# A token-mixing trunk on one core: ScalarE empties the banks of r, k, v and of the convolution's input, the scan's output moves into another tile, modulation steps are split, and the steps stand in a new order

## The chip, the cores and the metric

The kernel runs on one core of a Trainium2 chip. The metric is device microseconds of one execution, the median of three runs. TensorE (PE in the profile) multiplies matrices and writes PSUM, VectorE (DVE) and ScalarE (ACT) do elementwise work and read PSUM, GpSimd (POOL) does elementwise work in SBUF, and SyncE (SP) issues most DMAs.

## The reference, cut to what matters

One layer on 512 tokens of width 1024, in fp32. The hidden state `h` is projected by one wide matrix to the inputs of three branches; then the gated result goes through `w_out`, and a squared-ReLU MLP of width 4096 follows.

```python
h = _rms_norm(x, norm_mix_gain[l]) * (1.0 + sc_m) + sh_m
proj = h @ w_comb                                   # 1024 -> 7424 columns
rwkv_in = _token_shift(proj[..., :N_SHIFT], mu_shift[l])   # p + (p_prev - p) * mu
conv_in = proj[..., N_SHIFT:N_SHIFT + 2 * D_CONV]
gates = jax.nn.sigmoid(proj[..., N_SHIFT + 2 * D_CONV:N_COLS])
y_a, v_first = _rwkv7_time_mix(rwkv_in, ...)        # r, k, v, decay, a, g; a state per head, step by step
y_b = _conformer_conv(conv_in, ...)                 # u1 * sigmoid(u2), 31 taps per channel, layer norm, silu
merged = jnp.concatenate([y_a, y_b], axis=-1) * gates
x = x + gt_m * (merged @ w_out[l])
h = _rms_norm(x, norm_ffn_gain[l]) * (1.0 + sc_f) + sh_f
x = x + gt_f * (jnp.square(jax.nn.relu(h @ w_ff_in[l])) @ w_ff_out[l])
return _rms_norm(x, final_gain)
```

## The kernel before, in words

**Projections.** Channels lie on the 128 partitions and the 512 tokens along the free axis. Each projection of 128 columns (`proj`) loads its weights, splits them into a high and a low half (`hi` cast on ScalarE, L151; `lo` subtracted on GpSimd or, where the step carries a "v", on VectorE, L152), and runs 24 matmuls of 128x512 into one PSUM bank: for each of 8 blocks of the inner dimension high times high (L175), high times the low half of h (L176) and low times high (L177). The pool of banks for projections has two (tag `pp`), so a third projection starts only when the first one's bank has been read by all that read it.

**Who empties a bank.** For r, k and v, `shift` reads the bank twice: ScalarE writes `(1-mu)*p` to SBUF (L469), then VectorE adds `mu*p` of the token before, read from the bank (L470). In `conv_tile`, ScalarE takes tanh of `ps_u2` (L779), and VectorE multiplies by `ps_u1`, read from its bank (L781). So VectorE's turn decides when these banks come free.

**The scan.** The 16 heads form 8 pairs and 4 quarters of two pairs. `rkv_pair` and `prep_pair` make a pair's operands, among them `tr` (L543), the sum over a head's channels `pb` (a matmul, L545) and its product with v, `bo` (L547). `products`, `solve` (rank-one steps on VectorE, L602 into `tmp`, L604 from `X`), `merge_inverses` (into a tile `RT` whose corner GpSimd clears, L636) and `scan` follow for each quarter; the scan's output `yq` is normalized in `group_norm` and goes to DRAM. The convolution's 30 taps (`conv_taps`, L788) are VectorE instructions of 128x512, started by ScalarE's `cz` (L786); four transposes (`pz`, L793) and `bn_stats` follow.

**The tail of this part.** `gate_a` multiplies the scan's output with its gate (gate tanh L819, a small matmul `pg` L821 with weights `wg`), `gate_b` does so for the convolution (`z`, with a Silu on ScalarE), results are reloaded, and `wo_step` runs one sixteenth of `w_out`. A modulation half (`mod_half`, then four small matmuls in `mod_cols`) sums eight rows of the conditioning matrix on VectorE. The MLP behind it is not touched.

**What sets the order.** The string `ORDER` lists the steps: U a convolution projection pair, R a pair's r, k, v, I products, V solve, O scan operands, M merge, S scan, Y group norm, T taps, N the convolution's norm, G and B the gates, L a reload, W a step of `w_out`, A a modulation half, Q the gate's spread. The number behind a colon moves a step's instructions ahead in the priorities of the framework's list scheduler, which then fixes the instruction order of every engine when the kernel is built; "v" puts the step's `lo` on VectorE.

Of the kernel before, what the change touches and what calls it, by code (L numbers as in the profile page):

```python
# [8 lines left out]
F32 = mybir.dt.float32  # L9
# [9 lines left out]
P = 128  # L19
T = 512  # L20
# [43 lines left out]
def tile_rwkv7_conformer(  # L64
# [143 lines left out]
    def mod_half(dst, seg, h, eng):  # L208

        n, tag = (3, "aacc") if x1 else (1, "w1")  # L210
        acc = tpool[0].tile([P, 512], F32, tag=tag, name=f"aacc{seg}{h}", bufs=1)
        for k in range(KT):
            mod_part(acc, seg, h, k, eng, n)
        return acc
# [32 lines left out]
    pq = cq.enter_context(tc.tile_pool(name="pq", bufs=1, space=PSUM, reuse_waits="tile"))  # L247
    early = {}
    lo_eng = [G]

    with tc.tile_pool(name="e1", bufs=1) as e1, tc.tile_pool(name="e2", bufs=2) as e2:
        xt = e1.tile([P, NT, D], F32, name="xt")
# [32 lines left out]
        ss = e1.tile([P, NT], F32, name="ss")  # L285
        rs = e1.tile([P, NT], F32, name="rs")
        sst = e1.tile([P, NT], F32, name="sst")
        sq = e1.tile([P, D], F32, name="sq")
        for tt in range(NT):
            S.activation(sq, xt[:, tt, :], AF.Square, accum_out=ss[:, tt:tt + 1])  # L290
        rstd_rows(rs, ss, 1.0 / D, 1e-6, sst)
# [165 lines left out]
    with ExitStack() as c1:  # L457
# [50 lines left out]
        def prep_pair(j, rt, kt, vv, sg, WA):  # L508
# [33 lines left out]
            V.tensor_tensor(AR[:, :, C:P], chunks(rt), Pt[:, :, 1:65], op=ALU.mult)  # L542
            V.scalar_tensor_tensor(rt, rt, VEC["r_k"][:, jc], kt, op0=ALU.mult, op1=ALU.mult)  # L543
            pb = pq.tile([P, T], F32, tag="m", name=f"pb{j}", bufs=2)
            PE.matmul(pb, blk1, rt, start=True, stop=True)  # L545
            bo = tp.tile([P, T], F32, tag="w1", name=f"bo{j}")
            V.tensor_tensor(bo, pb, vv, op=ALU.mult)  # L547
# [83 lines left out]
        def merge_inverses(q, d1, d2):  # L631


            RT = xq.tile([P, 16, C], F32, tag="RT", name=f"RT{q}", bufs=2)
            for pr in range(2):
                G.memset(RT[64 * pr + 32:64 * pr + 64, :, 0:32], 0.0)  # L636
            W = xq.tile([P, 7, 8, 32], F32, tag="U", name=f"W{q}")
# [42 lines left out]

        def scan(q, prs, RVs, RT):

            yq = qp.tile([P, NCHK, 2, C], F32, tag="yq", name=f"yq{q}")
            st = qp.tile([P, NCHK, 2, 6], F32, tag="st", name=f"st{q}")
            HP = [slice(0, 64), slice(64, 128)]
            HEADS = [(p, e) for e in range(2) for p in range(2)]
# [87 lines left out]
        def conv_tile(j):  # L774
            ps2 = proj(U2 + j * P, f"u2_{j}")
            tp = tpool[0]
            gl = tp.tile([P, CW - 1 + T], F32, tag="gl", name=f"gl{j}", bufs=2)
            G.memset(gl[:, 0:CW - 1], 0.0)
            S.activation(gl[:, CW - 1:], ps2, AF.Tanh, scale=0.5)  # L779
            ps1 = proj(U1 + j * P, f"u1_{j}")  # L780
            V.scalar_tensor_tensor(gl[:, CW - 1:], gl[:, CW - 1:], 1.0, ps1, op0=ALU.add, op1=ALU.mult)  # L781
            return gl

        def conv_taps(j, gl):
            cz = tpool[0].tile([P, T], F32, tag="cz", name=f"cz{j}")
# [27 lines left out]
        def gate_a(j):  # L813
            tp = tpool[0]
            wg = tp.tile([P, P], F32, tag="wg", name=f"wg{j}")
            nc.sync.dma_start(out=wg, in_=w_gate_up[0][:, j * P:(j + 1) * P])
            ps = proj(GA + j * P, f"ga{j}")
            ga = tp.tile([P, T], F32, tag="ga", name=f"gat{j}")
            S.activation(ga, ps, AF.Tanh, scale=0.5)  # L819
            pg = pp.tile([P, T], F32, tag="o", name=f"pg{j}")  # L820
            PE.matmul(pg, wg, sgl, start=True, stop=True)  # L821
            V.scalar_tensor_tensor(ga, ga, 1.0, pg, op0=ALU.add, op1=ALU.mult)
            gy = tp.tile([P, T], F32, tag="gy", name=f"gy{j}")
            nc.sync.dma_start(out=gy, in_=yad[j])
            V.scalar_tensor_tensor(ga, gy, VEC["gn_bias"][:, j:j + 1], ga, op0=ALU.add, op1=ALU.mult)
            merged(j, ga, 1.0)
# [165 lines left out]
        def step(op):  # L992
# [14 lines left out]
            elif k == "Y":  # L1007
                group_norm(i, quarters[i], *scans[i])
                if i == 3:
                    enter_tail()  # L1010
            elif k == "U":
                scans["gl", i] = conv_tile(i)
            elif k == "T":
                conv_taps(i, scans.pop(("gl", i)))
            elif k == "G":
                gate_a(i)
            elif k == "N":
                scans["cn"] = conv_norm()
            elif k == "B":
                gate_b(i, *scans["cn"])  # L1020
            elif k == "L":
                reload()
            elif k == "A":
                seg, h = 2 + i // 2, i % 2
                acc = mod_half(modt[seg - 2], seg, h, V)
                mod_cols(pp, "o", modt[seg - 2], acc, seg, h)
            elif k == "Q":
                spread(tail["m2"], tail["p2"], "m", gate[0], modt[0], "gm")
            elif k == "W":
                wo_step(int(wn[0] == 16))  # L1030
# [142 lines left out]
```

## Time and profile before

| | |
|---|---|
| median of 3 runs | 1107.88 us (1107.52, 1107.88, 1110.65) |
| profiled execution, its own time | 1106.56 us |
| its span | 1104.8 us |
| mean granted TensorE clock | 0.971 of full speed |
| TensorE busy | 1011.8 us (92% of the span) |
| VectorE busy | 772.9 us (70%) |
| ScalarE busy | 496.3 us (45%) |
| GpSimd busy | 181.2 us (16%) |

The span runs from the first to the last instruction in the profile; the execution's own time is 1.8 us more. A busy share is a mean over the whole span; the projections and the scan lie in the first half of it, and the MLP, which fills TensorE without a gap, in the second.

### The profile page before, as it was taken

To read this page: it belongs to the slowest core of one execution; us is meant where nothing else is said; L and a number is where in the kernel's file an instruction comes from. 1 tells how busy PE (TensorE), PEld (TensorE's weight loads), DVE (VectorE), ACT (ScalarE), POOL (GpSimd) and SP (SyncE) were. 2 spreads that over 40 slices of the span, in tenths; PEclk is the share of its full clock that TensorE was granted. 3 is DMA by queue.
4 is the path that set the end of the run, shared out by engine and by line. 5 is a ranking of instruction groups with operands and counts; after the bars stand their busy time and mean duration, and the time that the engine had idled before them with its cause. 6 is when DMAs were issued, how large, how long until landed. Compare 5 with 4: busy or idle time off the path is not lost.

```text
span 1104.8 us, 18962 instructions
## 1 busy us (share of the span) xinstructions
PE 1011.8 (92%) x7061; PEld 777.7 (70%) x7061; DVE 772.9 (70%) x1525; ACT 496.3 (45%) x980; POOL 181.2 (16%) x188
## 2 busy tenths in 40 slices
PE   3999889998999799996996998999999999999995
PEld 1877666666667576664664776788788888888884
DVE  4869996899569897898665776776555445445557
ACT  5546455745765367344352343363224323423432
POOL 2113044233314441301012022100000000000012
PEclk9999999999999899997898999999999999999998
DMA  9522333222214322323257785623523333323331
GB/s 333 177 72 85 94 86 98 57 60 58 90 37 134 100 60 83 88 75 118 82 180 232 227 264 162 192 84 111 156 87 96 94 92 100 96 94 98 96 105 76
DMA packets 178215, 127.82 MB, mean 116 GB/s; under 512 B 43033, under 2 KB 146891, under 8 KB 178123
## 3 DMA queue, kind: packets, MB, share of 16 engines
q1 hardware_dynamic: 178123, 126.62, 38.1%
q8 instruction: 55, 0.90, 0.3%
q14 instruction: 37, 0.30, 0.1%
HBM read 113.73 MB, written 12.85 MB: 115 GB/s over the span
## 4 chain that ended last, share of the span: by engine, by line
PE 49%; DVE 28%; DMA 10%; ACT 6%; issue 5%; SPq 1%; POOL 1%; DVEq 0%; ACTq 0%; POOLq 0%
DVE cz L788 9%; PE ps_fi L177 5%; PE ps_fi L176 5%; PE ps_fi L175 5%; PE acc_fo L1048 4%; PE acc_fo L1047 4%; PE acc_fo L1046 4%; DMA ar<-in_ada_w_dram 3%; DVE aacc L222 2%; DVE X L604 2%; PE pA L185 2%; DVE tmp L602 2%; DMA mr<-mgd 2%; PE ps_u L177 1%; PE ps_u L176 1%
## 5 line engine op out<-in xcount | busy, mean ns | idle before, releaser
L788 DVE SCALAR_TENSOR_TENSOR cz<-gl,cw,cz 128x512 f32<-128x512 f32 x240 | 199.0, 829 | 3.4 <-ACT cz L786 0.3
L175 PE MATMUL ps_fi<-hh,hi_fi 128*128 128x512 f32 (+1 forms) x288 | 105.7, 367 | 0.0
L176 PE MATMUL ps_fi<-hl,hi_fi 128*128 128x512 f32 (+1 forms) x288 | 105.6, 367 | 0.0
L177 PE MATMUL ps_fi<-hh,lo_fi 128*128 128x512 f32 (+1 forms) x288 | 105.4, 366 | 0.0
L1046 PE MATMUL acc_fo<-hi_fo,fh 128*128 128x512 f32 x256 | 101.2, 395 | 0.0
L1047 PE MATMUL acc_fo<-lo_fo,fh 128*128 128x512 f32 x256 | 101.0, 395 | 0.0
L1048 PE MATMUL acc_fo<-hi_fo,fl 128*128 128x512 f32 x256 | 100.9, 394 | 0.0
L152 DVE TENSOR_TENSOR lo_fo<-raw_fo,hi_fo 128x512 fp32r<-128x512 f32 x64 | 44.2, 691 | 77.0 <-ACT hi_fo L151 76.9
L151 ACT CAST hi_fo<-raw_fo 128x512 fp32r<-128x512 f32 x64 | 39.7, 621 | 108.4 <-PE acc_fo L1048 86.9
L152 DVE TENSOR_TENSOR lo_fi<-raw_fi,hi_fi 128x512 fp32r<-128x512 f32 x64 | 43.9, 690 | 48.1 <-ACT hi_fi L151 47.1
L151 ACT CAST hi_fi<-raw_fi 128x512 fp32r<-128x512 f32 x64 | 39.8, 622 | 76.9 <-PE ps_fi L176 48.8
L1064 POOL TENSOR_TENSOR x<-x,fgain 128x512 f32<-128x512 f32 x4 | 5.5, 1393 | 375.9 <-ACT sq L1058 375.9
L222 DVE SCALAR_TENSOR_TENSOR aacc<-ar,cact,aacc 128x512 f32<-128x512 f32 x56 | 51.6, 922 | 13.8 <-DMA ar<-in_ada_w_dram 13.4
L177 PEld LDWEIGHTS ps_fi<-hh,lo_fi 128*128 128x128 f32 x288 | 54.3, 189 | 8.7
L176 PEld LDWEIGHTS ps_fi<-hl,hi_fi 128*128 128x128 f32 x288 | 54.3, 189 | 8.6
L175 PEld LDWEIGHTS ps_fi<-hh,hi_fi 128*128 128x128 f32 x288 | 54.3, 189 | 8.6
L152 POOL TENSOR_TENSOR lo_u<-raw_u,hi_u 128x512 fp32r<-128x512 f32 x28 | 40.6, 1458 | 94.6 <-ACT hi_u L151 40.7
L1048 PEld LDWEIGHTS acc_fo<-hi_fo,fl 128*128 128x128 f32 x256 | 48.2, 188 | 11.1
L1047 PEld LDWEIGHTS acc_fo<-lo_fo,fh 128*128 128x128 f32 x256 | 48.2, 188 | 10.9
L1046 PEld LDWEIGHTS acc_fo<-hi_fo,fh 128*128 128x128 f32 x256 | 48.2, 188 | 10.9
L175 PE MATMUL ps_u<-hh,hi_u 128*128 128x512 f32 x128 | 53.3, 416 | 2.3 <-DVE lo L470 2.3
L177 PE MATMUL ps_u<-hh,lo_u 128*128 128x512 f32 x128 | 54.6, 427 | 0.3 <-POOL lo_u L152 0.3
(386 smaller groups left out, 2495.4 us busy)
## 6 DMA issues: line engine op xcount, KB each, us to landing
ar<-in_ada_w_dram SPq DMA_DIRECT2D x64, 256.0 KB
raw_fi<-in_w_ff_in_dram SPq DMA_DIRECT2D x64, 256.0 KB
raw_fo<-in_w_ff_out_dram SPq DMA_DIRECT2D x64, 256.0 KB
araw<-in_ada_w_dram SPq DMA_DIRECT2D x8, 1024.0 KB
raw_u<-in_w_in_dram SPq DMA_DIRECT2D x32, 256.0 KB
raw_wo<-in_w_out_dram SPq DMA_DIRECT2D x32, 256.0 KB
raw_k<-in_w_in_dram SPq DMA_DIRECT2D x16, 256.0 KB
raw_v<-in_w_in_dram SPq DMA_DIRECT2D x16, 256.0 KB
```

The lines of the kernel that those rows point to most:

```text
L151: S.copy(hi, raw)
L152: (eng or V).tensor_tensor(lo, raw, hi.bitcast(F32), op=ALU.subtract)
L175: PE.matmul(ps[:, ts_], wh[:, i, :], mh[:, k, ts_], start=first, stop=False, skip_group_check=True)
L176: PE.matmul(ps[:, ts_], wh[:, i, :], ml[:, k, ts_], start=False, stop=False, skip_group_check=True)
L177: return PE.matmul(ps[:, ts_], wl[:, i, :], mh[:, k, ts_], start=False, stop=(k == KT - 1), skip_group_check=True)
L185: last_mm[0] = PE.matmul(*a, **kw).ins
L222: eng.scalar_tensor_tensor(acc, a, cact[:, k:k + 1], acc, op0=ALU.mult, op1=ALU.add)
L602: V.tensor_tensor(tv, X[:, 0:n, s:s + 1].to_broadcast([P, n, m]), U[:, s:s + 1, s + 1:16].to_broadcast([P, n, m]), op=ALU.mult)
L788: V.scalar_tensor_tensor(cz, gl[:, w:w + T], cw[:, w * KT + j:w * KT + j + 1], cz, op0=ALU.mult, op1=ALU.add)
L1046: PE.matmul(acc[tt], fh[:, k, ts_], wh, start=(n == 0), stop=False)
L1047: PE.matmul(acc[tt], fh[:, k, ts_], wl, start=False, stop=False)
L1048: return PE.matmul(acc[tt], fl[:, k, ts_], wh, start=False, stop=(n == KT - 1))
```

## The change

ScalarE copies the bank of each r, k and v projection into a new tile `ev` (two buffers), and VectorE reads `ev` in its place; the same for `ps_u1` with `evu`. That is 24 + 8 ScalarE copies of 128x512 more, and 32 VectorE instructions that read two SBUF tiles in place of a bank and a tile. The scan's output becomes the second half of the inverses' tile RT, which is twice as wide, so that the eight memsets on GpSimd clear twice the columns. `x1`, which shares RT's two buffers, is loaded when these are free. Step A is split into A (the sum on VectorE, with two buffers in the tail) and C (the four matmuls). `fill` can put spare matmuls (high times high, 128x512, the result is never read) ahead of a step; the new order asks for 8 and 6 of them, at two W steps. Some steps of `ORDER` change place and many their number or their "v": on balance one `lo` instruction fewer falls to VectorE, while R1's six go to GpSimd early on and four of U6's come to VectorE later.

```diff
-    "U1:0v R0:0v R1:0v I0 U4 R2:0v R3 V0 I1:200 U3:50 T1:500 M0 O0 T4 S0:50 U2 V1 M1 T3:2000 Y0 R4 R5 G0 "
-    "O1:200 T2 U6:100 I2:1000 V2:500 G1 S1:500 T6 U7 M2 R6 R7 O2 T7 Y1 I3:1000 V3:1000 U5 S2:100 T5:100 "
...
+    "U1:0v R0:0v R1 I0 U4 R2:0v R3 V0 I1:200 U3:50 T1:200 M0 O0 T4 S0:50 U2 V1 M1 T3:2000 Y0 R4 R5 "
+    "O1:200 G0 U6:100v T2 I2:1000 V2:500 G1:0v S1:500 M2 T6 U7 R6 R7 O2 T7 Y1 I3:50 V3:1000 U5 S2:100 O3 "
...
+    "W:100 W:0v+8 W:1000 W:2000 W:1000v W:1000+6 L:1000 W:200 A5:2000 C5 W A1:1000 C1 W:0v Q:500 W:200 "
...
-        acc = tpool[0].tile([P, 512], F32, tag=tag, name=f"aacc{seg}{h}", bufs=1)
+        acc = tpool[0].tile([P, 512], F32, tag=tag, name=f"aacc{seg}{h}", bufs=2 if x1 else 1)
...
+    def fill(ps):
+
+        for _ in range(spare.pop(0) if spare else 0):
+            PE.matmul(ps, hh[:, 0, 0:P], hh[:, 0, :], start=True, stop=True, skip_group_check=True)
...
-        sq = e1.tile([P, D], F32, name="sq")
+        sq = xq.tile([P, D], F32, tag="U", name="sq")
...
         def shift(dst, ps, m):
             S.activation(dst, ps, AF.Copy, scale=om[:, m:m + 1])
+            if m < 24:
+
+                ev = tp.tile([P, T], F32, tag="ev", name=f"ev{m}", bufs=2)
+                S.copy(ev, ps)
+                ps = ev
             V.scalar_tensor_tensor(dst[:, 1:T], ps[:, 0:T - 1], VEC["mu"][:, m:m + 1], dst[:, 1:T],
                                    op0=ALU.mult, op1=ALU.add)
...
-            RT = xq.tile([P, 16, C], F32, tag="RT", name=f"RT{q}", bufs=2)
+            RT = xq.tile([P, 32, C], F32, tag="RT", name=f"RT{q}", bufs=2)
...
-            yq = qp.tile([P, NCHK, 2, C], F32, tag="yq", name=f"yq{q}")
+            yq = RT[:, 16:32, :].rearrange("p (c h) n -> p c h n", h=2)
...
             ps1 = proj(U1 + j * P, f"u1_{j}")
-            V.scalar_tensor_tensor(gl[:, CW - 1:], gl[:, CW - 1:], 1.0, ps1, op0=ALU.add, op1=ALU.mult)
+            ev = tp.tile([P, T], F32, tag="ev", name=f"evu{j}", bufs=2)
+            S.copy(ev, ps1)
+            V.scalar_tensor_tensor(gl[:, CW - 1:], gl[:, CW - 1:], 1.0, ev, op0=ALU.add, op1=ALU.mult)
...
+            if spare and spare[0]:
+                fill(tail["p2"].tile([P, 512], F32, tag="m", name=f"fill{h}{n}"))
...
-                acc = mod_half(modt[seg - 2], seg, h, V)
-                mod_cols(pp, "o", modt[seg - 2], acc, seg, h)
+                scans["a", i] = mod_half(modt[i // 2], 2 + i // 2, i % 2, V)
+            elif k == "C":
+                mod_cols(pp, "o", modt[i // 2], scans.pop(("a", i)), 2 + i // 2, i % 2)
```

On TensorE the instructions stand as before up to the projection `ps_u1_1`, and nearly so from `ps_gb0` to `ps_ga7`. Three places have moved in ways that matter below.

**VectorE, while the second quarter's operands are made.** `X0` and `tmp0` are the first solve, `cz4` the taps of convolution tile 4, `bo2` the product that ends pair 2, `tv3` and `tr3` the shifts of pair 3's v and r. Before:

```order
L788 SCALAR_TENSOR_TENSOR cz4_2014<-gl4_1077,cw_83,cz4_2014 128x512
L604 TENSOR_TENSOR X0_1463<-X0_1463,tmp0_1464 128x5x11
L788 SCALAR_TENSOR_TENSOR cz4_2014<-gl4_1077,cw_83,cz4_2014 128x512
L547 TENSOR_TENSOR bo2_1284<-pb2_1282,tv2_1208 128x512
L602 TENSOR_TENSOR tmp0_1464<-X0_1463,U0_1461 128x60
L788 SCALAR_TENSOR_TENSOR cz4_2014<-gl4_1077,cw_83,cz4_2014 128x512
L604 TENSOR_TENSOR X0_1463<-X0_1463,tmp0_1464 128x6x10
L602 TENSOR_TENSOR tmp0_1464<-X0_1463,U0_1461 128x63
L604 TENSOR_TENSOR X0_1463<-X0_1463,tmp0_1464 128x7x9
L602 TENSOR_TENSOR tmp0_1464<-X0_1463,U0_1461 128x64
L604 TENSOR_TENSOR X0_1463<-X0_1463,tmp0_1464 128x8x8
```

After (the lines of the functions lie about 13 further down, L803 is the tap, L482 the shift, L615 and L617 the solve):

```order
L803 SCALAR_TENSOR_TENSOR cz4_2044<-gl4_1091,cw_83,cz4_2044 128x512
L560 TENSOR_TENSOR bo2_1306<-pb2_1304,tv2_1226 128x512
L615 TENSOR_TENSOR tmp0_1492<-X0_1491,U0_1489 128x63
L803 SCALAR_TENSOR_TENSOR cz4_2044<-gl4_1091,cw_83,cz4_2044 128x512
L617 TENSOR_TENSOR X0_1491<-X0_1491,tmp0_1492 128x7x9
L803 SCALAR_TENSOR_TENSOR cz4_2044<-gl4_1091,cw_83,cz4_2044 128x512
L615 TENSOR_TENSOR tmp0_1492<-X0_1491,U0_1489 128x64
L803 SCALAR_TENSOR_TENSOR cz4_2044<-gl4_1091,cw_83,cz4_2044 128x512
L617 TENSOR_TENSOR X0_1491<-X0_1491,tmp0_1492 128x8x8
L803 SCALAR_TENSOR_TENSOR cz4_2044<-gl4_1091,cw_83,cz4_2044 128x512
L482 SCALAR_TENSOR_TENSOR tv3_1403<-ev19_1405,vt_81,tv3_1403 128x511
L615 TENSOR_TENSOR tmp0_1492<-X0_1491,U0_1489 128x63
```

Of the 30 taps of `cz4`, 29 stood ahead of `bo2`; now 7 stand ahead of it, and 23 behind it, the first of them each behind a step of the solve; `tv3` reads `ev19` instead of the bank of `ps_v3`.

**TensorE, at the transposes of the first convolution tile.** `cz1` is the result of its 30 taps, `ps_u1_4`, `ps_r2` and `ps_k3` are projections. Before:

```order
L175 MATMUL ps_u1_4_1092<-hh_100,hi_u1_40_1082 128x512
L176 MATMUL ps_u1_4_1092<-hl_101,hi_u1_40_1082 128x512
L177 MATMUL ps_u1_4_1092<-hh_100,lo_u1_40_1083 128x512
L793 MATMUL pz1_1689<-ident_63,cz1_1656 128x128 x4
L175 MATMUL ps_u1_4_1092<-hh_100,hi_u1_40_1082 128x512
L176 MATMUL ps_u1_4_1092<-hl_101,hi_u1_40_1082 128x512
L177 MATMUL ps_u1_4_1092<-hh_100,lo_u1_40_1083 128x512
```

After, where the same transposes stand (L809 now) and what stands around them:

```order
L176 MATMUL ps_r2_1243<-hl_101,hi_r21_1239 128x512
L177 MATMUL ps_r2_1243<-hh_100,lo_r21_1240 128x512
L525 MATMUL pl2_1273<-tri_66,sg2_1139 128x128 x4
L533 MATMUL pa2_1283<-lo2_606,WA2_1135 128x512
L809 MATMUL pz1_1719<-ident_63,cz1_1686 128x128 x4
L175 MATMUL ps_k3_1336<-hh_100,hi_k30_1326 128x512
L540 MATMUL pn2_1289<-w1_2_1287,blk1_65 128x512
L176 MATMUL ps_k3_1336<-hl_101,hi_k30_1326 128x512
L177 MATMUL ps_k3_1336<-hh_100,lo_k30_1327 128x512
```

The transposes `pz1` stood inside the projection `ps_u1_4`; now they stand behind the projection `ps_r2` and pair 2's small matmuls. Of pair 3, the sum `pb3` moved behind 17 more matmuls of the projections `ps_u1_3` and `ps_u2_2`, and `pb2` behind two more of `ps_v3` (22 in place of 20).

**TensorE, between the last `gate_a` and the fifth `gate_b`.** Before:

```order
L175 MATMUL ps_ga7_6501<-hh_100,hi_ga71_6497 128x512
L176 MATMUL ps_ga7_6501<-hl_101,hi_ga71_6497 128x512
L177 MATMUL ps_ga7_6501<-hh_100,lo_ga71_6498 128x512
L175 MATMUL ps_gb4_6555<-hh_100,hi_gb40_6545 128x512
L176 MATMUL ps_gb4_6555<-hl_101,hi_gb40_6545 128x512
L177 MATMUL ps_gb4_6555<-hh_100,lo_gb40_6546 128x512
```

After, where L255 is the spare matmul:

```order
L176 MATMUL ps_ga7_6561<-hl_101,hi_ga71_6557 128x512
L177 MATMUL ps_ga7_6561<-hh_100,lo_ga71_6558 128x512
L255 MATMUL fill05_6994<-hh_100 128x512 x8
L255 MATMUL fill09_7075<-hh_100 128x512 x6
L175 MATMUL ps_gb4_6615<-hh_100,hi_gb40_6605 128x512
L176 MATMUL ps_gb4_6615<-hl_101,hi_gb40_6605 128x512
```

All 14 spare matmuls stand together, behind the projection of `ps_ga7` and ahead of the one of `ps_gb4`. The small matmul `pg7`, which stood behind 12 of the 24 matmuls of `ps_gb1`, now stands behind all of these and 12 of the first `w_out` step, 24 matmuls further on.

## Rows read from the trace of the kernel before

**Rows 1.** the page's head and its busy shares (busy us, share of the span, instructions)
```profile
span 1104.8 us, 18962 instructions
PE 1011.8 (92%) x7061; PEld 777.7 (70%) x7061; DVE 772.9 (70%) x1525; ACT 496.3 (45%) x980; POOL 181.2 (16%) x188
```

**Rows 2.** stretches of the span: busy us and count by engine, granted clock, DMA
```profile
core 0: us, PE busy (x) PEld busy (x) DVE busy (x) ACT busy (x) POOL busy (x), PEclk, DMA share, GB/s
80.00:120.00 40.00, 36.89 (x153) 27.80 (x152) 38.01 (x56) 21.77 (x32) 11.16 (x14) 0.96 0.31 91
120.00:160.00 40.00, 37.61 (x201) 27.93 (x199) 38.82 (x57) 24.59 (x47) 11.54 (x11) 1.00 0.34 83
160.00:200.00 40.00, 34.75 (x331) 25.39 (x333) 26.75 (x51) 18.43 (x36) 13.44 (x16) 0.91 0.34 90
...
320.00:360.00 40.00, 38.65 (x250) 29.60 (x248) 33.49 (x75) 23.61 (x57) 14.57 (x12) 1.00 0.39 102
360.00:400.00 40.00, 30.48 (x487) 23.18 (x486) 36.50 (x58) 17.78 (x30) 14.33 (x17) 0.91 0.30 80
...
560.00:600.00 40.00, 33.44 (x157) 23.81 (x156) 23.87 (x48) 17.47 (x38) 10.56 (x8) 0.96 0.69 217
sum 520.00, PE 471.09 PEld 339.41 DVE 426.36 ACT 276.68 POOL 135.24; mean PE 36.24 PEld 26.11 DVE 32.80 ACT 21.28 POOL 10.40
800.00:960.00 160.00, 160.00 (x712) 131.05 (x711) 79.87 (x132) 53.28 (x89) 0.00 (x0) 1.00 0.31 93
```

**Rows 3.** timeline, TensorE: matmuls that waited, and steps behind one wait
```profile
113.92 0.65 PE L793 MATMUL pz<-ident,cz 128*128 128x128 f32 x4 [2.85 <-DVE cz L788]
162.81 1.84 PE L545 MATMUL pb<-tr,blk 128*128 128x512 f32 x2 [4.86 <-DVE tr L543]
186.66 1.80 PE L545 MATMUL pb<-tr,blk 128*128 128x512 f32 x2 [2.38 <-DVE tr L543]
370.63 0.77 PE L175 MATMUL ps_v<-hh,hi_v 128*128 128x512 f32 x1 [7.21 <-DVE X L604]
371.62 0.63 PE L177 MATMUL ps_v<-hh,lo_v 128*128 128x512 f32 x1
...
374.18 0.63 PE L177 MATMUL ps_v<-hh,lo_v 128*128 128x512 f32 x1
...
586.70 0.80 PE L175 MATMUL ps_gb<-hh,hi_gb 128*128 128x512 f32 x1 [4.11 <-ACT gat L819]
602.39 1.10 PE L821 MATMUL pg<-sgl,wg 128*128 128x512 f32 x2 [3.92 <-DMA wg<-in_w_gate_up_dram]
```

**Rows 4.** timeline around that wait: VectorE, then ScalarE
```profile
369.80 0.68 DVE L781 SCALAR_TENSOR_TENSOR gl<-gl,ps_u 128x512 f32<-128x512 f32 x1
374.30 0.72 ACT L526 ACTIVATE w<-tk,vt 128x512 f32<-128x512 f32 x1 [9.82 <-DVE tk L470]
```

**Rows 5.** durations by line, ns min/median/max, and the page's mean for L788
```profile
L470 DVE SCALAR_TENSOR_TENSOR tr<-ps_r,vt,tr x8: 743/746/750, 80.8 to 418.4; 128x511 f32<-128x511 f32 x8
L781 DVE SCALAR_TENSOR_TENSOR gl<-gl,ps_u x8: 679/689/690, 72.5 to 470.5; 128x512 f32<-128x512 f32 x8
L788 DVE SCALAR_TENSOR_TENSOR cz<-gl,cw,cz x240: 730/752/1805, 74.1 to 524.9; 128x512 f32<-128x512 f32 x120
L788 DVE SCALAR_TENSOR_TENSOR cz<-gl,cw,cz 128x512 f32<-128x512 f32 x240 | 199.0, 829 | 3.4 <-ACT cz L786 0.3
L152 DVE TENSOR_TENSOR lo_r<-raw_r,hi_r x6: 678/682/693, 67.5 to 138.1; 128x512 fp32r<-128x512 f32 x6
L636 POOL MEMSET RT<- x8: 516/518/521, 3.2 to 328.7; 32x512 f32 x8
L779 ACT ACTIVATE gl<-ps_u x8: 577/595/601, 67.3 to 459.1; 128x512 f32<-128x512 f32 x8
```

**Rows 6.** who waited for whom on VectorE, 400 to 480 us
```profile
DVE gl L781 <- PE ps_u L177: 3.0, 1, 3.0
```

More of the change, by code (lines that the diff above doesn't have):

```diff
@@ L249, in tile_rwkv7_conformer @@
     lo_eng = [G]
+    spare = []
+    def fill(ps):
+        for _ in range(spare.pop(0) if spare else 0):
+            PE.matmul(ps, hh[:, 0, 0:P], hh[:, 0, :], start=True, stop=True, skip_group_check=True)
     with tc.tile_pool(name="e1", bufs=1) as e1, tc.tile_pool(name="e2", bufs=2) as e2:
@@ L464, in proj @@
             ps = pp.tile([P, T], F32, tag="pp", name=f"ps_{nm}", bufs=2)
+            fill(ps)
             mm3(ps, w, (hh, hl))
@@ L544, in prep_pair @@
             pb = pq.tile([P, T], F32, tag="m", name=f"pb{j}", bufs=2)
+            fill(pb)
             PE.matmul(pb, blk1, rt, start=True, stop=True)
@@ L791, in conv_taps @@
             pz = pp.tile([P, NT, P], F32, tag="o", name=f"pz{j}")
+            fill(pz.rearrange("p a b -> p (a b)"))
             for tt in range(NT):
@@ L820, in gate_a @@
             pg = pp.tile([P, T], F32, tag="o", name=f"pg{j}")
+            fill(pg)
             PE.matmul(pg, wg, sgl, start=True, stop=True)
@@ L1023, in step @@
             elif k == "A":
-                seg, h = 2 + i // 2, i % 2
-                acc = mod_half(modt[seg - 2], seg, h, V)
-                mod_cols(pp, "o", modt[seg - 2], acc, seg, h)
+                scans["a", i] = mod_half(modt[i // 2], 2 + i // 2, i % 2, V)
+            elif k == "C":
+                mod_cols(pp, "o", modt[i // 2], scans.pop(("a", i)), 2 + i // 2, i % 2)
             elif k == "Q":
@@ L1033, in tile_rwkv7_conformer @@
             op, hp = (op + ":0").split(":")[:2]
+            hp, wm = (hp + "+").split("+")[:2]
             lo_eng[0] = V if hp.endswith("v") else G
+            spare[:] = [int(n) for n in wm]
             with ahead(int(hp.rstrip("v"))):
```

9 rows, old and new, of the table ORDER are left out of this document.

## The prediction

> **What bounds the kernel now.** I read the page's head first, to see which engine could be the limit [rows 1]: TensorE is busy 1011.8 us of 1104.8, the others well below. That share is a mean over two halves, so next I cut the span into stretches [rows 2]. From 800 to 960 us TensorE works without a gap: 712 matmuls in 160 us, 0.2247 us a step. The change doesn't touch that half, and nothing in it can be won. In the first half it is otherwise: from 80 to 600 us TensorE is busy 471.1 of 520 us, VectorE 426.4 and ScalarE 276.7. From 80 to 160 us VectorE is busy 38.0 and 38.8 of 40 us, that is, it has hardly a gap, and TensorE has 36.9 and 37.6. So in this half TensorE waits for VectorE here and there, and a change that helps must shorten VectorE's chain or let TensorE pass it.
>
> Third, TensorE's own line, for each matmul that waited long [rows 3]. The reader is to see six waits and who ended them:
> - 2.85 us at 113.92, the transposes `pz`, for the taps `cz`;
> - 4.86 us at 162.81 and 2.38 us at 186.66, the sum `pb`, for `tr` on VectorE;
> - 7.21 us at 370.63, the first matmul of a projection `ps_v`, for VectorE. The row names X, a step of the solve. What that matmul needs is a free bank, and VectorE's reading of one, `gl`, ends at 369.80 + 0.68 = 370.48 us, just ahead of the matmul [rows 4]. So I take it that TensorE stood for 7 us because VectorE came late to a bank that was long full;
> - 4.11 us at 586.70, the gate projection `ps_gb`, for the gate on ScalarE;
> - 3.92 us at 602.39, the small matmul `pg`, for its weights by DMA.
>
> Behind a wait TensorE also runs slower. From 371.62 to 374.18 us it makes six steps in 2.56 us, 0.427 us a step [rows 3], against 0.2247 at full clock; the granted clock of that stretch is 0.91, of 80 to 120 us 0.96, of 160 to 200 us 0.91 and of 560 to 600 us 0.96 [rows 2]. These are the levels of 2.4 and 1.2 GHz, so a stretch of 40 us at a mean of g has (1-g) x 40 / 0.5 us at the lower one: 3.2, 7.2, 7.2 and 3.2 us for 0.96, 0.91, 0.91 and 0.96. Half of that is what the work there would have saved at the full clock, where TensorE has work to do.
>
> **The change part by part.** All sums are made against the profiled execution, 1106.56 us, whose span is 1104.8; the median of the runs shown lies 1.3 us above it.
>
> *Stretch 80 to 200 us.* The order takes all three waits from where they are: `pz1` stands behind a whole projection and more, `pb2` behind two and `pb3` behind 17 more matmuls, and R1's six `lo`, at 0.682 us each 4.1 us [rows 5], leave VectorE for GpSimd. The waits are 2.85 + 4.86 + 2.38 = 10.1 us, the lower clock there costs (3.2 + 7.2) / 2 = 5.2: 15.3 us at most. But VectorE is busy 38.0 + 38.8 + 26.8 = 103.6 of 120 us and TensorE 109.3 [rows 2], and 15 us less would leave 105 us to both: VectorE would be at 99.5 / 105 = 95% even without the six `lo`. Two engines that feed each other do not both run at 95%. What is late next is `bo2`: 22 taps that stood ahead of it are put behind it, into 160 to 200 us, where VectorE had 13.2 us idle. I take 8 us, about half; bounds 0 and 15.3.
>
> *Stretch 320 to 480 us.* With `ev` and `evu` the bank is read by ScalarE alone. The wait of 7.21 us and half of 7.2 us at the lower clock are 10.8 us. But VectorE is busy 33.5 of 40 us before and 36.5 during that stretch [rows 2], and its work isn't less: the copy lets TensorE run ahead, up to the point where TensorE needs what VectorE still has to make (`pb`, the scan's operands, the solve). What VectorE itself loses to TensorE in this part is one wait of 3.0 us for `ps_u` at 400 to 480 us [rows 6]. VectorE's chain can be shortened by that, and by no more; the rest of TensorE's gain would be spent in the next wait. I take 3 us; bounds 0 and 10.8.
>
> *560 to 605 us.* The 14 spare matmuls cost 14 x 0.2247 = 3.15 us where nothing hides them. They stand where TensorE waited 4.11 us, so I count them as nothing, and if that wait is gone they cost 3.15. Running through the wait, they may also keep the clock up, which is worth at most half of 3.2, 1.6 us. `pg7` now has 24 more matmuls, 24 x 0.2247 = 5.4 us, ahead of it, and it waited 3.92 us for its weights, whose load stands as early as before. Together at most 5.5 us; I take 4; bounds 5.5 and a loss of 3.15.
>
> *The 32 instructions that read SBUF twice.* The shift takes 0.746 us from a bank (0.743 to 0.750), the product of the convolution 0.689 [rows 5]. No row shows either with two tiles in SBUF. The nearest is the tap, of the same kind and size: at least 0.730, median 0.752, but up to 1.805 and 0.829 in the mean [rows 5]. I take the mean: 32 x (0.829 - 0.746) = 2.7 us on VectorE; bounds 0 (the tap's median) and 32 x (1.805 - 0.746) = 33.9 us. By the tap's median alone the term would be 32 x 0.006 = 0.2 us and the time 1093. The Trainium skill, page "SBUF — State Buffer", section "Who interferes with whom", speaks for the mean: VectorE and GpSimd share one pair of ports under an exclusive lock, so an instruction with a second input in SBUF can meet GpSimd where one that reads PSUM does not. The rows agree: eight reads of PSUM within 7 ns of one another, taps in SBUF up to 1.8 us.
>
> *The 32 copies on ScalarE.* The nearest row is its tanh of a bank of the same size, 0.595 us [rows 5]: 32 x 0.595 = 19.0 us. ScalarE is idle 520 - 276.7 = 243 us in this part, so I take 0; bound 19.0 if each stands on the path. What is queued behind them are the casts `hi` of the next projections and the scan's small copies `Rs`, for which TensorE waits; the copy also comes behind the first reading of the bank, so a bank is free two ScalarE instructions, some 1.2 us, after its last matmul, in place of one of ScalarE and VectorE's turn.
>
> *Edits at nothing.* The memsets of RT, 8 x 0.518 = 4.1 us more [rows 5], lie on GpSimd, busy 135 of 520 us. The split of A into A and C moves the same four matmuls; the later load of the second half of `x1` has until the first `w_out` result, over 100 us on. `yq` in RT changes the lifetime of a buffer of which there are two, and M and S of neighbouring quarters use them in turn; that could hold a merge up, and I have no row to price it but the memset's own place.
>
> The sum: 8 + 3 + 4 - 2.7 = 12.3 us less, 1106.56 - 12.3 = 1094.3 for such an execution, and 1.3 above it as a median: 1095.6, say 1095.
>
> **The rivals.** A measurement of this kernel tells a change from none at about 0.3%, 3.3 us.
>
> *Full gain.* Every wait listed and the clock behind it are won: 15.3 + 10.8 + 5.5 = 31.6 us, less 2.7, so about 1079 as a median. Against it speaks VectorE at 95% and more in the stretch it would have to shorten. Chance 0.10.
>
> *The waits only move.* VectorE is the limit of the first half in truth: its chain of shifts, taps and solve steps ends when it ended before, TensorE waits elsewhere for the same. Then only the tail's 4 us and VectorE's loss of 2.7 remain: 1.3 us less, about 1106.6. For it: 38 of 40 us in two stretches. Against it: 13.2 us idle at 160 to 200 us. Chance 0.18.
>
> *ScalarE's copies on the path (slower).* The copies stand in ScalarE's order ahead of casts and of the scan's copies, and TensorE pays for each: the gains of 8 + 3 + 4 = 15, less 19.0 for the copies and 2.7 for the double reads, is a loss of 6.7 us, about 1114.6. It decides from (15 - 2.7) / 0.595 = 21 of the 32 copies on. For it: ScalarE's `w` waited 9.82 us for VectorE at 374.30 [rows 4], so ScalarE's queue does stand behind VectorE at times, and a copy that stands behind such a wait holds the bank just as VectorE did. Against it: 243 us idle. Chance 0.17. The Trainium skill says something on this side too, page "VectorE: DVE Perf Modes", section "Rules for kernel authors": work on a matmul's output should either accept reading PSUM or copy to SBUF first where many operations follow. Here one operation follows each copy, so by that rule the copies are a plain addition; no row here shows a copy that paid off or did not.
>
> **How the numbers follow.** My own case, a part of each gain, has the remaining 0.55 and spans 1087 to 1103: the 3.15 of the spare matmuls and 4 us of the first two stretches the one way, half of what is left between 15 and 31.6 us, 8.3, the other way. Its middle is the prediction. The range of 8 in 10 takes in the waits that only move and the lower half of the slower case, and leaves most of the full gain out, some 0.17 together: 1081 to 1115. Faster by over 0.3% means below 1104.6: 0.55 + 0.10 = 0.65. Same is the second rival, 0.18; slower the third, 0.17.
>
> **What would show it.** In the changed kernel's trace: the waits of `pz` and `pb` between 80 and 200 us gone and VectorE's busy time from 160 to 200 us above 30 of 40; the wait of a projection for VectorE near 370 us replaced by a copy on ScalarE, and TensorE waiting soon after for `pb`, `tr` or the solve; the shifts' mean above 0.75 us with single ones over 1 us; the spare matmuls inside a gap at 580 to 590 us and `pg7` without a wait. What would make it wrong: a mean of the shifts over 1.2 us (32 x 0.45 = 14 us, the whole gain); TensorE's waits for `hi` or for `Rs` rising by over 10 us; a merge that waits for RT; or a new wait of VectorE for a copy `ev` that is queued late on ScalarE.

## The result, and the profile after

The changed kernel is slower: 1124.12 us median (1122.77 to 1125.7), against 1108.8 us for the kernel before in the same comparison; the ratio is 1.0156, with a 95% interval of 1.0131 to 1.0181. The forecast was 1095 us. The profiled execution took 1123.2 us, 16.6 us more than that of before.

The page's head and busy shares of the changed kernel [rows 1 of before]:

```profile
span 1121.2 us, 19001 instructions
PE 1013.9 (90%) x7075; PEld 780.9 (70%) x7075; DVE 779.6 (70%) x1524; ACT 509.4 (45%) x1012; POOL 199.0 (18%) x189
```

TensorE's busy time grew by 2.1 us only, and the span by 16.4: TensorE waits more. VectorE has 6.7 us more work. The same stretches as in [rows 2], busy time and count by engine, granted clock, DMA:

```profile
80.00:120.00 40.00, 33.50 (x133) 24.97 (x132) 36.69 (x45) 22.06 (x34) 18.30 (x18) 0.87 0.25 71
120.00:160.00 40.00, 39.62 (x212) 29.80 (x211) 23.96 (x42) 27.01 (x51) 8.41 (x8) 1.00 0.41 105
160.00:200.00 40.00, 30.61 (x121) 22.28 (x119) 39.55 (x65) 16.44 (x26) 19.97 (x17) 0.89 0.25 70
...
320.00:360.00 40.00, 39.93 (x373) 28.10 (x372) 27.91 (x85) 19.63 (x50) 1.29 (x1) 1.00 0.26 63
360.00:400.00 40.00, 32.76 (x291) 25.27 (x292) 34.06 (x60) 19.00 (x40) 21.49 (x18) 0.91 0.42 117
400.00:440.00 40.00, 32.72 (x363) 24.59 (x349) 36.25 (x47) 24.23 (x43) 15.19 (x13) 0.91 0.21 60
560.00:600.00 40.00, 39.39 (x284) 28.23 (x282) 25.54 (x65) 21.77 (x49) 6.08 (x5) 1.00 0.51 163
```

From 120 to 160 us TensorE is nearly full, with VectorE at 24 us; from 160 to 200 us VectorE is full, and TensorE falls to 30.6. So the work has moved, and TensorE's waits with it. The granted clock of 80 to 120 us, the stretch with the longest of the waits below, fell from 0.96 to 0.87. TensorE's timeline shows the waits that count now, in place of those of [rows 3], and the spare matmuls:

```profile
100.24 2.08 PE L558 MATMUL pb<-tr,blk 128*128 128x512 f32 x2 [6.50 <-DVE tr L555]
...
167.26 1.95 PE L558 MATMUL pb<-tr,blk 128*128 128x512 f32 x2 [3.92 <-DVE tr L555]
...
197.61 2.08 PE L558 MATMUL pb<-tr,blk 128*128 128x512 f32 x2 [5.47 <-DVE tr L555]
...
425.02 2.07 PE L558 MATMUL pb<-tr,blk 128*128 128x512 f32 x2 [5.12 <-DVE tr L555]
...
598.40 3.70 PE L255 MATMUL fill<-hh 128*128 128x512 f32 x14
602.48 0.50 PE L175 MATMUL ps_gb<-hh,hi_gb 128*128 128x512 f32 x1 [0.37 <-ACT gat L835]
```

The waits of `pz` at 113.92 and of a projection at 370.63 are gone. But `pb` waits long for `tr` four times, 6.50 + 3.92 + 5.47 + 5.12 = 21.0 us. The 14 spare matmuls take 3.70 us where `ps_gb` had waited 4.11 us, and it still waits 0.37 us behind them, so that gap was there to fill.

### The profile page after: what moved, and what is told of

The parts are those of the page before. It is cut to its first block, busy times and chain, and to the rows that moved or that the text cites. A ratio compares the mean times of both kernels' runs of the same rounds, so it can differ in the third digit from the quotient of the medians.

```text
span 1121.2 us, 19001 instructions
## 1 busy us (share of the span) xinstructions
PE 1013.9 (90%) x7075; PEld 780.9 (70%) x7075; DVE 779.6 (70%) x1524; ACT 509.4 (45%) x1012; POOL 199.0 (18%) x189
## 4 chain that ended last, share of the span: by engine, by line
PE 35%; DVE 9%; DMA 7%; ACT 3%; issue 2%; SPq 1%; POOL 0%; DVEq 0%; ACTq 0%; POOLq 0%
PE ps_fi L176 5%; PE ps_fi L175 5%; PE ps_fi L177 5%; PE acc_fo L1069 4%; PE acc_fo L1068 4%; PE acc_fo L1067 4%; DMA ar<-in_ada_w_dram 3%; DVE cz L803 1%; DVE aacc L222 1%; DMA raw_wo<-in_w_out_dram 1%; DMA raw_fo<-in_w_ff_out_dram 1%; DMA mr<-mgd 1%; DMA z<-czd 1%; PE ps_gb L175 1%; PE ps_ga L175 1%
## 5 line engine op out<-in xcount | busy, mean ns | idle before, releaser
L803 DVE SCALAR_TENSOR_TENSOR cz<-gl,cw,cz 128x512 f32<-128x512 f32 x240 | 198.3, 826 | 4.2 <-ACT cz L801 1.5
L151 ACT CAST hi_fi<-raw_fi 128x512 fp32r<-128x512 f32 x64 | 39.6, 621 | 73.5 <-PE ps_fi L176 49.0
L222 DVE SCALAR_TENSOR_TENSOR aacc<-ar,cact,aacc 128x512 f32<-128x512 f32 x56 | 49.0, 875 | 14.3 <-DMA ar<-in_ada_w_dram 13.8
L998 PE MATMUL acc_wo<-hi_wo,mh 128*128 128x512 f32 x128 | 50.1, 404 | 4.2 <-ACT hi_wo L151 2.6
```

The lines of the kernel that those rows point to most:

```text
L151: S.copy(hi, raw)
L222: eng.scalar_tensor_tensor(acc, a, cact[:, k:k + 1], acc, op0=ALU.mult, op1=ALU.add)
L998: PE.matmul(wacc[h][tt], mh[k][:, ts_], wh, start=(n == 0), stop=False)
```

## The experiments

All times are medians beside the kernel before on the same chip (whose median lies between 1104.71 and 1108.8 us, by the chip), so the ratios are what is compared.

**First theories.** Theory 1: the new order is at fault (taps and GpSimd's `lo` against the pairs' chains). Theory 2: the copies are.

*old_order*, the changed code with the old string, in which each A is followed at once by its C and no spare matmuls are asked for:

```diff
-    "U1:0v R0:0v R1 I0 U4 R2:0v R3 V0 I1:200 U3:50 T1:200 M0 O0 ...
+    "U1:0v R0:0v R1:0v I0 U4 R2:0v R3 V0 I1:200 U3:50 T1:500 M0 O0 ...
```

> The changed code (copies on ScalarE, scan output in RT, A split) with the step order of the kernel before; each A is followed at once by its C, no spare matmuls. Theory 1, the new order (where taps and GpSimd's lo stand against pair chains) makes the loss: 1105 to 1112 us, TensorE's waits of pb for tr back near 8 us. Theory 2, the copies on ScalarE make it (each late copy delays a shift): 1116 to 1125 us, waits of pb for tr above 15 us.

Measured: 1133.58 us, 1.0238 (1.0218 to 1.0258), slower than the changed kernel. TensorE's waits, 60 to 620 us, in total, number and longest:

```profile
PE pb L558 <- DVE tr L555: 14.3, 4, 7.0
PE pz L809 <- DVE cz L803: 11.1, 2, 7.0
```

*no_copies*, the new order with the banks read by VectorE as before:

```diff
-            if m < 24:
-                ev = tp.tile([P, T], F32, tag="ev", name=f"ev{m}", bufs=2)
-                S.copy(ev, ps)
-                ps = ev
...
-            ev = tp.tile([P, T], F32, tag="ev", name=f"evu{j}", bufs=2)
-            S.copy(ev, ps1)
...
```

> The changed kernel with the new order, but VectorE reads r, k, v and u1 from their banks again (no ev, no evu). Theory 1: 1119 to 1128 us, pb's waits for tr about 20 us. Theory 2: 1104 to 1112 us, these waits near 8 us.

Measured: 1122.87 us, 1.0143 (1.0108 to 1.0178). So either half alone makes a slow kernel, and neither theory holds by itself.

*no_fill* leaves out the spare matmuls (`W:0v+8` and `W:1000+6` become `W:0v` and `W:1000`):

> The changed kernel without the 14 spare matmuls. If they lie in a gap that stays, as the prediction had it: 1124, no change. If the gap has closed and they cost their 3.15 us: 1120 to 1122 us. If they hold the clock up and that matters, 1125 to 1127 us.

Measured: 1122.1 us, 1.0132 (1.0109 to 1.0154). The ratio is 0.0024 under that of the changed kernel, some 2.7 us, and the two intervals overlap: whether the 14 matmuls cost anything is not settled by this.

*r1_vector*, the changed kernel with `R1:0v` for `R1`:

> The changed kernel with the six lo of R1 back on VectorE (R1:0v). Theory 1 in the form that GpSimd's lo slow VectorE's taps there (five taps took 5.69 and four 5.06 us, where 0.75 us each is usual): the wait of pb near 100 us falls from 6.7 us to under 2 us, 1116 to 1121 us. Theory 2: 1123 to 1127 us, for six lo at 0.69 us come back to VectorE.

Measured: 1127.82 us, 1.0179 (1.0158 to 1.02). Slower, against theory 1 in this form; but the scheduler dealt the order anew (by the two traces at least 350 of the 7075 matmuls stand elsewhere in TensorE's order), so this does not judge the six `lo` alone.

**One part at a time, old string.** Theory 3: RT's longer life. Theory 4: any added instruction makes the scheduler deal another order, and that costs.

*rt_only*, the kernel before with the scan's output in RT and `sq` in the shared slot:

```diff
-            RT = xq.tile([P, 16, C], F32, tag="RT", name=f"RT{q}", bufs=2)
+            RT = xq.tile([P, 32, C], F32, tag="RT", name=f"RT{q}", bufs=2)
...
-            yq = qp.tile([P, NCHK, 2, C], F32, tag="yq", name=f"yq{q}")
+            yq = RT[:, 16:32, :].rearrange("p (c h) n -> p c h n", h=2)
```

> The kernel before with one part of the change: the scan's output in the second half of RT (and sq in the shared slot), no copies, old order; the instruction order of every engine stays nearly as it was. Theory 3, that RT's longer life makes the merges or scans wait: 1113 to 1120 us. Theories 1, 2 and 4: 1106 to 1110 us, no change. Theory 4 is: any added instruction re-deals the order that the scheduler makes of the steps, and that costs 10 to 25 us, since the string fits the old instructions only.

Measured: 1107.42 us, 1.001 (0.9992 to 1.0027): no change. Theory 3 falls.

*copies_rkv* and *copies_u* add to that the first or the second half of the copies:

> Old order, with the 24 copies of r, k and v alone (and RT as changed; u1 is read from its bank). If the copies' cost of 26 us with the old order goes by their number (theory 2): about 24/32 of it, 1124 to 1130 us. Theory 4, the re-dealt order: 1115 to 1130 us, with TensorE's waits at other places than with all 32.

> Old order, with the 8 copies of u1 alone. By number (theory 2): about 8/32 of 26 us, 1111 to 1116 us. Theory 4: far more than its share, 1118 to 1130 us, since here too the order changes by some 1000 places.

Measured: 1125.99 us, 1.0186 (1.0151 to 1.022) with 24 copies, 1121.74 us, 1.0145 (1.0112 to 1.0178) with eight. Eight copies are 8 x 0.58 = 4.6 us of ScalarE and cost 16 us: far more than their share of 26. The 24 fit both theories; the eight speak for theory 4.

*order_only* is the kernel before with the new string and A split, nothing else:

> The kernel before with the new order of steps alone (no copies, no spare matmuls, scan output in its own tile; A still split into A and C). Theory 1, the new order is at fault by itself: 1119 to 1124 us, as without the copies. Theory 4 says the same, since the new order was not made for these instructions. Theory 3: 1108 to 1114 us.

Measured: 1123.97 us, 1.0181 (1.0132 to 1.0229). As theories 1 and 4 had it.

**Places held.** To part the copies from the order that they cause, the next kernels fix each engine's order by issue-order edges between neighbours, taken from the built program of another kernel. Only the copies are left free, and the scheduler puts them where they are ready. In the traces of these kernels TensorE, VectorE and GpSimd run the same instructions on the same tiles in the same order as in *rt_only* (the new places: as in the changed kernel), and ScalarE too but for the copies, so *rt_only* is the old places without a copy. With all 32 copies at the old places `ev` and `evu` have one buffer each, where the change has two; ScalarE's copies waited 0.2 us in all for VectorE to free one.

```diff
+        run = [mine[k] for k in places]
+        for a, b in zip(run, run[1:]):
+            tc.add_manual_dep(b, a.name, no, reason="keep_order")
```

> All 32 copies (and RT as changed, one buffer ev and one evu), but with every other instruction held to the place on its engine that it has without the copies, in the old order: issue-order edges fix it, only the copies are let in. Theory 2, the copies' own work and waits cost the 26 us: 1122 to 1134 us. Theory 4, the copies cost by the order that the scheduler makes with them: 1098 to 1110 us; the wait of 7.2 us of a projection for VectorE near 370 us should then be gone or shorter.

> The 24 copies of r, k and v alone, all other instructions held to their old places. Theory 2: 1120 to 1128 us (as without the fixing). Theory 4: 1102 to 1110 us, and the wait near 370 us stays, since the bank of u1 is read by VectorE still.

> The 8 copies of u1 alone, all other instructions held to their old places. Theory 2: 1115 to 1123 us. Theory 4: 1098 to 1106 us, as the wait near 370 us (7.2 us and the lower clock behind it) is the one that these copies can take away.

> The changed kernel without the copies, every instruction held to the place that it has in the changed kernel. Theory 2: 1100 to 1112 us. Theory 4, the places make the loss: 1122 to 1135 us, at or above the changed kernel, since the copies can only help TensorE past VectorE's readings at the same places.

Measured: all 32 copies at the old places 1118.31 us, 1.0122 (1.0103 to 1.0141); the 24 alone 1113.83 us, 1.0072 (1.0049 to 1.0094); the eight alone 1113.35 us, 1.009 (1.0059 to 1.012); the new places without copies 1113.96 us, 1.0082 (1.0066 to 1.0098), and once more on another chip 1113.85 us, 1.0049 (1.0032 to 1.0067). All four lie between the ranges of the two theories. Theory 2 is right that copies cost by themselves, about half of what they cost with the old string, and theory 4 has the other half: 1.2% held, 2.4% when the order is dealt anew. The new places, spare matmuls included, cost 0.5 to 0.8% without any copy. So of the changed kernel's 1.56% the places make 0.5 to 0.8, and the copies at these places the rest, 0.7 to 1.1.

Where the early bank's gain goes shows in *u_old_places*. Its timeline, TensorE, around the place where 7.21 us were lost [rows 3]:

```profile
367.09 0.39 PE L176 MATMUL ps_v<-hh,hi_v 128*128 128x512 f32 x1
367.32 0.39 PE L177 MATMUL ps_v<-hl,hi_v 128*128 128x512 f32 x1
...
378.79 1.11 PE L805 MATMUL pz<-ident,cz 128*128 128x128 f32 x4 [7.46 <-DVE cz L799]
```

The projection starts without a wait, at 0.23 us a step, the full clock; then TensorE stands 7.46 us at the transposes of the next convolution tile, until VectorE's last tap. Before, it came to the same transposes at 376.75 us and did not wait. The copies only moved the place where TensorE waits for VectorE. In *rkv_old_places*, which leaves u1's bank to VectorE, the wait of 7.2 us near 370 us stays: it was a wait for that bank, as the prediction had read it.

**What a copy costs.**

```diff
                 SPARE.add(S.copy(ev, ps).ins.name)
-                ps = ev
```

> All 32 copies stand in ScalarE's queue, all else at the old places, but VectorE reads the bank as before, so nothing waits for a copy but the bank itself. If a copy costs by ScalarE's time alone (casts and the scan's copies behind it): 1115 to 1119 us, as with the copies read. If it costs because VectorE's shift waits for it, or by the second SBUF input: 1106 to 1111 us.

```diff
-                ev = tp.tile([P, T], F32, tag="ev", name=f"ev{m}", bufs=1)
-                SPARE.add(S.copy(ev, ps).ins.name)
-                ps = ev
+                ps = hh.bitcast(F32)[:, 0, :]
```

> No copies; VectorE's 32 instructions read a row of h in SBUF in place of the bank, so the token before is left out of r, k and v, and u1 out of the convolution; all else at the old places. The banks are free as soon as ScalarE is done, at no cost: the most that the change could bring by them. If the freed banks are worth the 7.2 us wait near 370 us and more: 1092 to 1100 us. If the gain goes into the next wait for VectorE's taps, as seen with the copies: 1103 to 1108 us. If the second SBUF input is what costs: 1109 to 1116 us.

Measured: *copies_unread* 1111.88 us, 1.0059 (1.0037 to 1.0082); *no_bank_read* 1114.29 us, 1.0068 (1.0043 to 1.0094). In *copies_unread* one thing was not as meant: the framework still lets VectorE's reading of a bank wait for the copy of it. VectorE's waits there, 60 to 560 us, in total, number and longest:

```profile
DVE gl L796 <- ACT evu L795: 8.8, 4, 3.6
...
DVE tv L482 <- ACT ev L481: 3.9, 4, 2.0
```

In *rt_only* the first of them is one for TensorE's `ps_u`, of 5.9 us. So 0.59% is the price of ScalarE's time and of the wait for it, with the bank held until VectorE has read it. The second SBUF input and the early release are not in it. They are what *copies_old_places* has on top, 1.22 - 0.59 = 0.63%, and what *no_bank_read* has by itself, with the banks freed early and no copy: 0.68%, slower all the same. Each of these ratios is good to some 0.2 or 0.3%. VectorE's 32 instructions there, busy time and mean ns, and the idle time ahead of them:

```profile
L481 DVE SCALAR_TENSOR_TENSOR tv<-hh,vt,tv 128x511 f32<-128x511 f32 x8 | 8.6, 1071 | 3.3 <-ACT tv L477 3.1
L481 DVE SCALAR_TENSOR_TENSOR tr<-hh,vt,tr 128x511 f32<-128x511 f32 x8 | 7.7, 959 | 2.6 <-ACT tr L477 2.6
...
L481 DVE SCALAR_TENSOR_TENSOR tk<-hh,vt,tk 128x511 f32<-128x511 f32 x8 | 7.0, 870 | 0.0
L793 DVE SCALAR_TENSOR_TENSOR gl<-gl,hh 128x512 f32<-128x512 f32 x8 | 5.9, 741 | 0.0
```

and in *rt_only*, where they read the banks:

```profile
L470 DVE SCALAR_TENSOR_TENSOR tv<-ps_v,vt,tv 128x511 f32<-128x511 f32 x8 | 6.0, 746 | 2.3 <-ACT tv L469 2.1
L470 DVE SCALAR_TENSOR_TENSOR tr<-ps_r,vt,tr 128x511 f32<-128x511 f32 x8 | 6.0, 746 | 3.0 <-ACT tr L469 3.0
L470 DVE SCALAR_TENSOR_TENSOR tk<-ps_k,vt,tk 128x511 f32<-128x511 f32 x8 | 5.9, 742 | 0.1
L781 DVE SCALAR_TENSOR_TENSOR gl<-gl,ps_u 128x512 f32<-128x512 f32 x8 | 5.5, 686 | 6.0 <-PE ps_u L177 5.9
```

29.2 us against 23.4: 5.8 us more on VectorE, and the kernel is 1114.29 - 1106.15 = 8.1 us slower. The 7.2 us wait near 370 us is gone here too, and the transposes wait 8.42 us at 380.32 in its place. In *copies_old_places* the same 32:

```profile
L483 DVE SCALAR_TENSOR_TENSOR tv<-ev,vt,tv 128x511 f32<-128x511 f32 x8 | 8.1, 1013 | 4.4 <-ACT ev L481 4.4
L797 DVE SCALAR_TENSOR_TENSOR gl<-gl,evu 128x512 f32<-128x512 f32 x8 | 6.5, 818 | 9.2 <-ACT evu L796 9.2
L483 DVE SCALAR_TENSOR_TENSOR tk<-ev,vt,tk 128x511 f32<-128x511 f32 x8 | 6.0, 748 | 1.9 <-ACT ev L481 1.7
L483 DVE SCALAR_TENSOR_TENSOR tr<-ev,vt,tr 128x511 f32<-128x511 f32 x8 | 6.0, 745 | 2.5 <-ACT ev L481 2.5
```

They take 26.6 us, 3.2 more than from banks. So the step from the bank to SBUF costs 0.63 to 0.68%, some 7 to 8 us, and the instructions' own longer time is 3.2 to 5.8 us of it. What the early release gives or costs lies in the same step and was not parted from it: no run frees a bank early and leaves VectorE one SBUF input.

**The new places.** *r1_new_places* holds all of the new places but puts R1's six `lo` on VectorE:

> The new places without the copies, all held, but R1's six lo on VectorE again. If GpSimd's lo against VectorE's taps make the first wait: pb's wait near 98 us under 1 us, and 4 to 6 us less than the same without it. If VectorE is the bound of this part and six lo more (4.1 us) fill what GpSimd frees: the same time within 2 us.

> The same kernel as no_copies_new_places, to stand beside r1_new_places: 1112 to 1116 us.

Measured: 1112.69 us, 1.005 (1.0031 to 1.007), beside 1.0049 without that edit. TensorE's first wait of `pb` falls from 4.53 to 3.37 us, no more, and the time is the same: GpSimd's `lo` for R1 are not the cause. The traces show why it comes out even. The six `lo` take 4.3 us more on VectorE, and with fewer of GpSimd's beside them the 30 taps from 60 to 130 us take 25.7 us, against 28.4 and 30.1 in the two traces without the edit. The waits of `pb` at the new places without copies, 60 to 620 us, then of *rt_only* and of the changed kernel:

```profile
PE pb L554 <- DVE tr L551: 17.4, 5, 4.5
```

```profile
PE pb L545 <- DVE tr L543: 8.0, 5, 4.9
```

```profile
PE pb L558 <- DVE tr L555: 21.6, 5, 6.5
```

The new places alone add 9.4 us of waiting for `tr`, the changed kernel has 4.2 more. Which of the moved taps and shifts make `tr` late was not taken apart and stays open.

**A version from the parts.** *old_head_new_tail* is the kernel before with the new string from behind Y3 on:

> The kernel before with the changed order from behind Y3 on alone (reloads, w_out steps, A and C apart with two sums in flight), no copies, no spare matmuls; the first 560 us stay in the old order. The changed kernel made good 6 us between 560 and 730 us with no copies at its places: 1098 to 1102 us. If that gain was only the gap that had opened ahead of it: 1104 to 1108 us.

Measured: 1104.86 us against 1106.15, 0.9981 (0.9963 to 1.0). The best of all, but by 0.2%, at the edge of what can be told from no change. It is the second expectation: what the changed kernel made good behind 560 us was for the most part the gap that had opened ahead of it.

## Why the prediction was wrong

Two of its terms had the wrong sign or size where it mattered: the copies, taken at nothing, and the new order's gain, taken at 8 us.

**The copies on ScalarE: taken as 0, bound 19.0.** This is the step that failed first. "ScalarE is idle 243 us in this part, so I take 0" read a share of idle time as cover. A copy lies between TensorE's last matmul and VectorE's reading, and VectorE waited for it. With all else at the old places the copies cost 0.59%, some 6.5 us, before VectorE reads them at all (*copies_unread*), and 1.22%, 13.6 us, when it does. VectorE's idle time ahead of its 32 readings there is 4.4 + 9.2 + 1.9 + 2.5 = 18.0 us, against 2.3 + 3.0 + 0.1 + 6.0 = 11.4 in *rt_only* above. In the changed kernel it is 6.8 + 0.4 + 6.3 + 6.8 = 20.3:

```profile
L796 DVE SCALAR_TENSOR_TENSOR gl<-gl,evu 128x512 f32<-128x512 f32 x8 | 8.4, 1046 | 6.8 <-ACT evu L795 6.7
L482 DVE SCALAR_TENSOR_TENSOR tk<-ev,vt,tk 128x511 f32<-128x511 f32 x8 | 7.3, 918 | 0.4 <-ACT ev L480 0.4
L482 DVE SCALAR_TENSOR_TENSOR tr<-ev,vt,tr 128x511 f32<-128x511 f32 x8 | 6.8, 854 | 6.3 <-ACT ev L480 6.3
L482 DVE SCALAR_TENSOR_TENSOR tv<-ev,vt,tv 128x511 f32<-128x511 f32 x8 | 6.1, 764 | 6.8 <-ACT ev L480 6.8
...
L795 ACT COPY evu<-ps_u 128x512 f32<-128x512 f32 x8 | 4.7, 581 | 0.4 <-PE ps_u L177 0.3
L480 ACT COPY ev<-ps_v 128x512 f32<-128x512 f32 x8 | 4.6, 578 | 0.5 <-DVE gl L796 0.5
```

Not all of the 20.3 is the copies': at the new places without them it is 5.7 + 4.9 + 0.1 + 4.7 = 15.4 us:

```profile
L478 DVE SCALAR_TENSOR_TENSOR tr<-ps_r,vt,tr 128x511 f32<-128x511 f32 x8 | 6.0, 747 | 5.7 <-ACT tr L477 5.7
L478 DVE SCALAR_TENSOR_TENSOR tv<-ps_v,vt,tv 128x511 f32<-128x511 f32 x8 | 6.0, 744 | 4.9 <-ACT tv L477 4.9
L478 DVE SCALAR_TENSOR_TENSOR tk<-ps_k,vt,tk 128x511 f32<-128x511 f32 x8 | 5.9, 742 | 0.1
L790 DVE SCALAR_TENSOR_TENSOR gl<-gl,ps_u 128x512 f32<-128x512 f32 x8 | 5.5, 684 | 4.7 <-PE ps_u L178 4.7
```

The copy's duration was right (0.595 us forecast, 0.58 measured). The slower rival had the copies on the path and gave 1114.6 us, but by another way: TensorE paying for casts and the scan's copies queued behind them. In *copies_old_places* TensorE's waits for `hi` are 0.7 us and for `Rs` 0.4, so that is not what happened. What happened stands only among the prediction's signs of being wrong, a wait of VectorE for a copy `ev`. The rival's time was also too low, since it let the gains of 15 us stand.

**The 32 double reads: 2.7 us forecast.** In the changed kernel they take 8.4 + 7.3 + 6.8 + 6.1 = 28.6 us, 5.2 more than the 23.4 from banks; at the old places 3.2 more with the copies and 5.8 without. The direction was right, the size too small. The Trainium skill, page "SBUF — State Buffer", section "Who interferes with whom", says that a VectorE instruction with two SBUF inputs contends with a GpSimd instruction that reads SBUF, and that one with at most one SBUF input, outside the two-port modes, does not. The runs agree: means of 0.742 to 0.746 us from a bank, 0.870 to 1.071 for the same three in *no_bank_read*. What was missed is that the whole step cost 7 to 8 us at the end, more than the instructions' own time.

**Stretch 320 to 480 us: 3 us forecast.** The wait of 7.21 us did go, as forecast, and what the prediction feared of the rest came in full: *u_old_places* and *no_bank_read* lose it again at once, at `pz`. No run shows a gain from this term.

**Stretch 80 to 200 us: 8 us forecast.** `pz` lost its wait, `pb` did not: it waits 6.50 + 3.92 + 5.47 = 15.9 us in that stretch in place of 4.86 + 2.38. The step "the order takes all three waits from where they are" counted how far TensorE's instruction moved, and not where VectorE's `tr` went. VectorE's 160 to 200 us went from 26.8 to 39.6 busy, as forecast, but the new places by themselves made the kernel 0.5 to 0.8% slower, 5.5 to 9 us, where this term and the tail's had 12 us of gain. This is the second step that failed. R1's `lo` on GpSimd, which the prediction counted as a relief, brought nothing that can be measured either way, for the taps beside them took longer by about as much.

**560 to 605 us: 4 us forecast.** Right in its parts: the spare matmuls lie in the gap, and `pg7` no longer waits long. The sum was too high: put by itself onto the kernel before, without the spare matmuls, the new last part is worth 0.2%, 1.3 to 2 us, with an interval that reaches no change.

**Edits at nothing.** RT, the memsets and the later load of `x1`: 1.001, as forecast. The split of A was not tried alone; in *old_head_new_tail* it costs nothing that can be seen.

**Not foreseen.** The order dealt anew. With the old string and all 32 copies the kernel is at 1.0238, and at 1.0122 with the places held: the scheduler's answer to the added instructions costs as much as the copies. The new string gets part of that back (1.0156). The old string is the better one for the instructions of the kernel before; with copies in it, it is the worse one.

"The waits only move" was the rival nearest in mechanism, and the slower rival in sign; neither had the order dealt anew, nor a new order that costs. The Trainium skill's page "VectorE: DVE Perf Modes", section "Rules for kernel authors", with its copy from PSUM only where many operations follow, is borne out here: one operation followed each copy, and the 32 copies cost 1.2% with everything else in place.

## What to carry to other kernels

Where two engines feed each other, the idle share of a third says nothing of what an instruction between them costs. Nor does its duration: here 32 x 0.58 = 18.6 us of copying cost some 6.5 us before anything read the copies, and the eight of u1, 4.6 us of copying, cost 8 to 10 us with their reading. What counts is whether the reader stands waiting: VectorE did for 11 of the 32 at the old places. Ask too which wait comes next on the engine that is freed. Before copying a bank to SBUF for its reader, try the reader on some other SBUF tile with no copy made: the bank is then free early, the second SBUF input is there, and if that is not faster, the copy is unlikely to be. And where a scheduler sets the order, hold the places when one part is tested: the edit and the order that it causes cost about the same here.

## What was not expected of the hardware

The early release of the banks, with no copy to pay for it, did not make up for the second SBUF input, although the profile showed 7.2 us of waiting for one bank. Eight copies of u1 (4.6 us on ScalarE) cost at least as much at the old places, 0.9%, as 24 of r, k and v, 0.7%. The traces say as much: VectorE loses 4.2 us to the eight (3.2 of idle time ahead of its readings, 1.0 of longer ones, against *rt_only*) and 3.7 us to the 24 (2.5 and 1.2), for it waits for four of the eight and for six of the 24. The kernels lost 8 to 10 us each, about twice that; the rest stays open.
